# Forget-gate series moved from GpSimd to VectorE, three operand splits moved between GpSimd and VectorE, and queries' parts moved by DMA

## Chip, cores and metric

One core of one Trainium2 chip. The metric is the device time of one execution in microseconds; the median of three runs of the kernel before is 821.5 us (821.19 to 821.72).

## What is computed

One step of a single hybrid encoder layer on 576 tokens: 512 prompt tokens, and 64 sample tokens that also look at a cache of 128. Eight heads use forgetting attention (running sums of log forget gates are added to the scores), eight heads use sparse attention (an indexer chooses the keys). Cut to what matters here:

```python
h = x @ w_in                                  # (576, 1024) @ (1024, 3376)
logf = log_sigmoid(fg + b_f)                  # 8 forget gates per token
cum  = cumsum(logf, axis=1)
# forgetting heads: softmax(q k^T / 8 + cum_q - cum_k, causal) v
# indexer: score = sum_h iw[h] * relu(iq[h] @ ik^T); keep the best topk keys
# sparse heads: softmax(q k^T / 8 over the kept keys) v
x = LN1(ALPHA * x + mix @ w_o)
x = LN2(ALPHA * x + relu(x @ w_up)**2 @ w_down)
y = x + sigmoid(x @ w_g + b_g) * (pe @ w_ple)
# outputs: y, and the new rows k, v, logf, idx_k
```

All matmuls are float32 in precision: each operand is split into a high part and a low part (value less high part), and three products are summed.

## The kernel before

The layer is worked on transposed: model columns lie on the 128 partitions, the 576 tokens along the free axis in two halves of 288. The 16 heads are handled in 8 pairs, p = 0 to 3 of the forgetting kind, p = 4 to 7 of the sparse kind. `proj(p)` projects a pair in the order k, q, v (k of pair 0 is done earlier, with the indexer's projection, in `idx_main`); each of the three is 48 matmuls into one PSUM tile `m`. While pair p+1 is projected, the attention of pair p runs between its matmuls: `drive` steps a main generator (one step is 6 matmuls), and after each step runs due work of `later`, the `fillers`, and a share of a background generator (the `ticks` with the stages `qk`, `addmax`, `exp`, `ptrans`, `pevac`, `pv`, `oevac`).

A weight unit is 128x1024. It is loaded by SP into one of three raw slots (`wraw`, line 163), its high part is made by ScalarE (`whl`, line 182), its low part by VectorE or, where `pool_l` is set, by GpSimd (line 186); a slot is free for the next load when the low parts are done. Each unit has two such pieces of 128x512.

The forget gates: `bg0` is the background of `proj(0)`. It calls `gates` (line 447) and `logf_part` (lines 525 to 547: log sigmoid by an exponential on ScalarE and a polynomial, results in `LF`), waits 8 steps, and calls `cum_part` (line 552: running sums by matmuls on `LF`); 3 steps later `cumT_part` transposes the sums and sends them by `gate_rows` (line 587) into the rows of `KLP` that the scores of `qk` (lines 811 and 813) read.

The indexer runs as a filler from the start of `proj(0)`: `idx_rest` rotates (`idx_rope`, lines 455 to 458), splits keys and queries (`zk_stack`, line 469; `zq_stack`, line 485) and transposes them on TensorE (lines 473, 490; evacuated at 474 and 492). Then `logit_jobs` multiplies head by head (line 601), with ReLU on ScalarE (line 606) and the weighted sum over heads on VectorE (lines 609 and 611). `choice` then selects the keys on VectorE by repeated maximum and replacement of eight (lines 631 and 633).

`proj_evac` evacuates a projection. For a query of p < 4 it makes two operands, QE (partitions 0 to 63 the high part of the even head, 64 to 127 its low part) and QO (the other way round): high parts by ScalarE (lines 680, 681), low parts by VectorE (682, 683), with copies into `Q2` by GpSimd (686, 687). For a key, the high part is moved to the other half by two DMAs (line 714) and the low part goes to `KLP` (lines 717, 718) by GpSimd, for p = 0 by VectorE. `v_out` transposes the values and splits them into `VHL` on GpSimd (lines 752, 753); their output is a DMA on SP (line 747).

Order within an engine: the program is written in the order above and then arranged by the language's scheduler, engine by engine; on the chip each engine, and SP's queue of DMA issues, takes its instructions in that fixed order.

Of the kernel before, what the change touches and what calls it, by code (L numbers as in the profile page):

```python
# [8 lines left out]
F32 = mybir.dt.float32  # L9
# [8 lines left out]
NS = 64  # L18
# [17 lines left out]
def tile_hybrid_step(ctx: ExitStack, tc: tile.TileContext, I, O):  # L36
# [287 lines left out]
    for p in range(8):  # L324
        for x, kind in enumerate("kqv"):
            U[kind, p] = WT.add(qkv[p * 3 + x], pool_l=(x < 2 and p > 1))
# [196 lines left out]
    def logf_part():  # L523
# [5 lines left out]
        w = sb.tile([128, 5, 8], F32, name="lg_w")  # L529
        ACT.activation(e, z, AF.Abs)  # L530
        ACT.activation(e, e, AF.Exp, scale=-1.0)
        DVE.tensor_scalar(w, z, 0.0, None, op0=OP.min)
        DVE.tensor_scalar(t, e, 2.0, None, op0=OP.add)
        DVE.reciprocal(t, t)
        POOL.tensor_tensor(t, t, e, OP.mult)
        POOL.tensor_tensor(t2, t, t, OP.mult)
        POOL.tensor_scalar(t, t, -2.0, None, op0=OP.mult)
        POOL.tensor_scalar(s, t2, 1.0 / 17, None, op0=OP.mult)
        for c in (15, 13, 11, 9, 7, 5, 3):
            POOL.tensor_scalar(s, s, 1.0 / c, None, op0=OP.add)  # L540
            POOL.tensor_tensor(s, s, t2, OP.mult)
        POOL.tensor_scalar(s, s, 1.0, None, op0=OP.add)
        POOL.tensor_tensor(s, s, t, OP.mult)
        POOL.tensor_tensor(LF[:, 0:4], s[:, 0:4], w[:, 0:4], OP.add)
        POOL.tensor_tensor(LF[:NS, 4:5], s[:NS, 4:5], w[:NS, 4:5], OP.add)
# [107 lines left out]
    def proj_evac(p, kind, m):  # L653
# [5 lines left out]
        def q(fn, d=None):  # L659
            if d is not None:  # L660
                dly[0] = d
            later(dly[0], fn)
# [14 lines left out]
        if g == 0:  # L677
            if kind == "q":
                P["q32s"] = sb.tile([128, NS], F32, name="q32s", bufs=2)
                q(lambda: ACT.mul(v2(QE[lo]), v[lo], sc))  # L680
                q(lambda: ACT.mul(v2(QO[hi]), v[hi], sc))
                q(lambda: DVE.scalar_tensor_tensor(v2(QE[hi]), v[lo], sc, f(v2(QE[lo])), op0=OP.mult, op1=OP.subtract))
                q(lambda: DVE.scalar_tensor_tensor(v2(QO[lo]), v[hi], sc, f(v2(QO[hi])), op0=OP.mult, op1=OP.subtract))
                q(lambda: ACT.mul(P["q32s"], m[:, 1, HW - NS:HW], sc))
                P["Q2"] = Q2[p % 2]
                q(lambda: POOL.tensor_copy(P["Q2"][lo, 0], f(QE[lo, :NP])))
                q(lambda: POOL.tensor_copy(P["Q2"][hi, 1], f(QO[hi, :NP])))
# [28 lines left out]
        eng = POOL if p else DVE  # L716
# [25 lines left out]
    def v_out(p):  # L742
# [9 lines left out]
        POOL.tensor_copy(VHL[:, :, :, 0, :], tv)  # L752
        POOL.tensor_tensor(VHL[:, :, :, 1, :], tv, f(VHL[:, :, :, 0, :]), OP.subtract)
# [200 lines left out]
    def bg0():  # L954
# [3 lines left out]
        for _ in range(8):  # L958
            yield 1
# [590 lines left out]
```

## Time and profile before

| | before |
|---|---|
| median of three runs | 821.5 us |
| profiled execution | 821.17 us |
| its span | 819.5 us |
| TensorE matmul busy | 797.4 us, 97% |
| VectorE busy | 569.3 us, 69% |
| ScalarE busy | 453.9 us, 55% |
| GpSimd busy | 131.5 us, 16% |

The span reaches from the first to the last instruction of the profiled execution; 1.7 us of its time lie outside. Engines are called PE (TensorE), DVE (VectorE), ACT (ScalarE), POOL (GpSimd) and SP, whose queue issues the DMAs; PEld is TensorE's loading of weights. L552 is line 552 of the kernel. Matmuls overlap in the pipeline, so a busy TensorE need not be one at its peak; a share of busy time is a mean over stages that have different limits. [...]

### The profile page before, as it was taken

How to read it: one execution, taken by the hardware profiler on the slowest of the kernel's cores; microseconds unless marked ns; L12 is line 12 of the kernel's file. 1: busy time of each engine (PE TensorE's matmuls, PEld its weight loads, DVE VectorE, ACT ScalarE, POOL GpSimd, SP SyncE). 2: the span in 40 equal slices, each digit the busy share in tenths (PEclk: the TensorE clock that was granted, in tenths of full speed). 3: DMA queues.
4: the chain of work that ended last, by engine and by line, in shares of the span. 5: the costliest groups of instructions: out<-in, count | busy, mean ns of one | idle time of the engine just before them, and what ended most of it. 6: DMA issues, size and time to landing. Idle time of an engine off the chain costs nothing.

```text
span 819.5 us, 15103 instructions
## 1 busy us (share of the span) xinstructions
PE 797.4 (97%) x5916; PEld 776.4 (95%) x5916; DVE 569.3 (69%) x1150; ACT 453.9 (55%) x965; POOL 131.5 (16%) x147
## 2 busy tenths in 40 slices
PE   7888999999999999999999999999999999999997
PEld 7877898989999999999999999999999999999997
DVE  6648999996646755889955947658485774737553
ACT  5537766588887954578532625345262543716451
POOL 8414252353350200120000000000000000012200
PEclk9979999999999999999999999999999999999999
DMA  8425122225322322442311414133131422631001
GB/s 290 163 9 137 67 57 87 79 77 195 115 69 73 112 65 78 155 163 83 129 52 54 121 34 142 64 103 100 55 106 52 129 78 83 239 108 48 23 31 64
DMA packets 29255, 79.68 MB, mean 97 GB/s; under 512 B 4864, under 2 KB 8704, under 8 KB 29056
## 3 DMA queue, kind: packets, MB, share of 16 engines
q1 hardware_dynamic: 29184, 78.72, 30.6%
q8 instruction: 46, 0.75, 0.4%
q14 instruction: 25, 0.20, 0.1%
HBM read 66.38 MB, written 9.54 MB: 93 GB/s over the span
## 4 chain that ended last, share of the span: by engine, by line
PE 82%; DVE 13%; ACT 2%; issue 1%; POOL 1%; DMA 1%; DVEq 0%; ACTq 0%
PE g L278 53%; PE m L278 15%; DVE dbias L633 3%; DVE m L631 3%; PE n L278 2%; DVE dbias L611 2%; PE V L897 2%; PE T L64 2%; DVE PT L878 1%; DVE sP L821 1%; PE S L416 1%; PE m L409 1%; PE m L416 1%; DVE whl L186 1%; PE S L813 1%
## 5 line engine op out<-in xcount | busy, mean ns | idle before, releaser
L182 ACT CAST whl<-wraw 128x512 fp32r<-128x512 f32 (+1 forms) x226 | 135.0, 611 | 160.2 <-PE g L278 149.1
L186 DVE TENSOR_TENSOR whl<-wraw,whl 128x512 fp32r<-128x512 f32 (+1 forms) x202 | 137.1, 697 | 68.5 <-ACT whl L182 67.5
L278 PE MATMUL g<-BH,whl 128*128 128x288 f32 (+2 forms) x864 | 181.7, 297 | 0.2 <-DVE Y L1205 0.2
L278 PE MATMUL m<-AH,whl 128*128 128x288 f32 x736 | 181.2, 312 | 0.0
L278 PEld LDWEIGHTS g<-BH,whl 128*128 128x128 f32 x864 | 141.1, 188 | 2.4 <-ACT u L1314 1.1
L278 PEld LDWEIGHTS m<-AH,whl 128*128 128x128 f32 x736 | 128.4, 191 | 1.3
L278 PE MATMUL g<-BL,whl 128*128 128x288 f32 (+2 forms) x432 | 127.2, 295 | 0.0
L278 PE MATMUL m<-AL,whl 128*128 128x288 f32 x368 | 110.4, 300 | 0.0
L278 PE MATMUL g<-hidE,whl 128*128 128x288 f32 (+2 forms) x768 | 103.6, 295 | 0.0
L278 PE MATMUL g<-hidO,whl 128*128 128x288 f32 (+2 forms) x768 | 103.3, 295 | 0.0
L278 PEld LDWEIGHTS g<-hidE,whl 128*128 128x128 f32 x768 | 102.3, 188 | 0.1
L278 PEld LDWEIGHTS g<-hidO,whl 128*128 128x128 f32 x768 | 102.3, 188 | 0.0
L278 PEld LDWEIGHTS g<-BL,whl 128*128 128x128 f32 x432 | 81.3, 188 | 0.1
L278 PEld LDWEIGHTS m<-AL,whl 128*128 128x128 f32 x368 | 70.6, 192 | 0.3
L278 PE MATMUL g<-s,whl 128*128 128x288 f32 x432 | 68.5, 298 | 0.0
L1097 POOL TENSOR_TENSOR ln_s<-Y 128x576 f32<-128x576 f32 (+2 forms) x3 | 4.6, 1546 | 383.7 <-DVE Y L1380 371.3
L278 PEld LDWEIGHTS g<-s,whl 128*128 128x128 f32 x432 | 60.1, 188 | 2.3 <-DVE u L1316 1.2
L829 ACT ACTIVATE sP<-sP,st 128x128 f32<-128x128 f32 (+4 forms) x72 | 39.7, 552 | 37.9 <-DVE st L821 37.7
L1355 DVE SCALAR_TENSOR_TENSOR Y<-Y,g 128x576 f32<-128x576 f32 x48 | 36.0, 751 | 21.6 <-PE g L278 21.1
L278 PE MATMUL m<-BH,whl 128*128 128x288 f32 x192 | 43.7, 304 | 0.0
L878 DVE TENSOR_TENSOR PT<-T,PT 128x128 fp32r<-128x128 f32 (+1 forms) x64 | 31.0, 484 | 16.3 <-ACT PT L877 15.8
L64 PE MATMUL T<-ident,sP 128*128 128x128 f32 (+1 forms) x176 | 31.3, 274 | 5.2 <-DVE PT L878 2.5
(276 smaller groups left out, 1353.5 us busy)
## 6 DMA issues: line engine op xcount, KB each, us to landing
wraw<-in_w_up_dram SPq DMA_DIRECT2D x32, 512.0 KB, 3.5
wraw<-in_w_down_dram SPq DMA_DIRECT2D x32, 512.0 KB, 3.5
wraw<-in_w_qkv_dram SPq DMA_DIRECT2D x23, 512.0 KB, 3.9
wraw<-in_w_gate_dram SPq DMA_DIRECT2D x8, 512.0 KB, 5.1
wraw<-in_w_o_dram SPq DMA_DIRECT2D x8, 384.0 KB, 3.1
out_vT_dram<-v SPq DMA_DIRECT2D x8, 288.0 KB, 2.1
Y<-in_xT_dram SPq DMA_DIRECT2D x8, 288.0 KB, 5.7
PLD<-PL SPq DMA_DIRECT2D x4, 576.0 KB, 2.8
```

The lines of the kernel that those rows point to most:

```text
L64: PE.transpose(out, in_, ident[:n, :n])
L182: ACT.copy(self.hv[h][0], src)
L186: eng.tensor_tensor(lv, src, f(hv), OP.subtract)
L278: PE.matmul(ps, W(w, kw, wc), a[:, ka, cols], start=(first and i == 0), stop=(last and i == n - 1))
L416: PE.matmul(acc[b][:n[b], :304], a[:, k, b * 128:b * 128 + n[b]], ixw(part, k), start=(k == 0 and i == 0), stop=(k == 7 and i == 2))
L611: DVE.scalar_tensor_tensor(dst[:n, :nk], r[:n, :nk], w, dst[:n, :nk], op0=OP.mult, op1=OP.add)
L631: DVE.max(m, s)
L633: DVE.match_replace(out=s, in_to_replace=m, in_values=s, imm_value=GONE)
L829: ACT.activation(j["P"], j["P"], AF.Exp, bias=j["st"][:, 0:1], scale=-1.0, accum_out=s)
L878: DVE.tensor_tensor(t[:, 1, :n, c], v, f(t[:, 0, :n, c]), OP.subtract)
L897: PE.matmul(ps[:, c], w, j["PT"][:, x, kb, c], start=(kb == 0 and x == 0), stop=(kb == i and x == 1))
L1355: later(0, lambda y=y, m=m, s=s: DVE.scalar_tensor_tensor(y, y, s, m[:, :, :HW], op0=OP.mult, op1=OP.add))
```

## The change

- `logf_part`: the absolute value is made on VectorE (a product with -1 and a maximum), not on ScalarE; the polynomial runs on VectorE, with addition and product in one instruction, not on GpSimd; the exponential stays on ScalarE.
- `bg0`: 11 steps instead of 8 before the running sums.
- Low parts of weights: GpSimd makes those of all units from 2q on (q and v of p = 2, all three of p = 3 to 7). Before it was k and q of p = 2 to 7.
- The low parts in `KLP` for p = 1 and the split of the values of p = 0 go from GpSimd to VectorE.
- Queries of p = 1 to 3: one ScalarE operation makes the high parts of both heads on 128 partitions, one VectorE operation the low parts, in the buffers t2 and t1; four DMAs on SP's queue move the quarters to QE and QO. The copies into `Q2` read the new tile.

```diff
@@ -323,7 +323,7 @@
     qkv, wup, wdown = tiles_of("w_qkv", 8), tiles_of("w_up", 8), tiles_of("w_down", 4)
     for p in range(8):
         for x, kind in enumerate("kqv"):
-            U[kind, p] = WT.add(qkv[p * 3 + x], pool_l=(x < 2 and p > 1))
+            U[kind, p] = WT.add(qkv[p * 3 + x], pool_l=(p * 3 + x > 6))
     for j, ap in enumerate(tiles_of("w_o6", 6)):
         U["o", j] = WT.add(ap)
     for k, ap in zip((6, 7), tiles_of("w_o2", 1)):
@@ -526,23 +526,20 @@
         t = sb.tile([128, 5, 8], F32, name="lg_t")
         t2 = sb.tile([128, 5, 8], F32, name="lg_t2")
         s = sb.tile([128, 5, 8], F32, name="lg_s")
-        w = sb.tile([128, 5, 8], F32, name="lg_w")
-        ACT.activation(e, z, AF.Abs)
+        DVE.tensor_scalar(e, z, -1.0, None, op0=OP.mult)
+        DVE.tensor_tensor(e, e, z, OP.max)
         ACT.activation(e, e, AF.Exp, scale=-1.0)
-        DVE.tensor_scalar(w, z, 0.0, None, op0=OP.min)
         DVE.tensor_scalar(t, e, 2.0, None, op0=OP.add)
         DVE.reciprocal(t, t)
-        POOL.tensor_tensor(t, t, e, OP.mult)
-        POOL.tensor_tensor(t2, t, t, OP.mult)
-        POOL.tensor_scalar(t, t, -2.0, None, op0=OP.mult)
-        POOL.tensor_scalar(s, t2, 1.0 / 17, None, op0=OP.mult)
+        DVE.tensor_tensor(t, t, e, OP.mult)
+        DVE.tensor_tensor(t2, t, t, OP.mult)
+        DVE.tensor_scalar(s, t2, 1.0 / 17, None, op0=OP.mult)
         for c in (15, 13, 11, 9, 7, 5, 3):
-            POOL.tensor_scalar(s, s, 1.0 / c, None, op0=OP.add)
-            POOL.tensor_tensor(s, s, t2, OP.mult)
-        POOL.tensor_scalar(s, s, 1.0, None, op0=OP.add)
-        POOL.tensor_tensor(s, s, t, OP.mult)
-        POOL.tensor_tensor(LF[:, 0:4], s[:, 0:4], w[:, 0:4], OP.add)
-        POOL.tensor_tensor(LF[:NS, 4:5], s[:NS, 4:5], w[:NS, 4:5], OP.add)
+            DVE.scalar_tensor_tensor(s, s, 1.0 / c, t2, op0=OP.add, op1=OP.mult)
+        DVE.scalar_tensor_tensor(s, s, 1.0, t, op0=OP.add, op1=OP.mult)
+        DVE.tensor_scalar(e, z, 0.0, None, op0=OP.min)
+        DVE.scalar_tensor_tensor(LF[:, 0:4], s[:, 0:4], -2.0, e[:, 0:4], op0=OP.mult, op1=OP.add)
+        DVE.scalar_tensor_tensor(LF[:NS, 4:5], s[:NS, 4:5], -2.0, e[:NS, 4:5], op0=OP.mult, op1=OP.add)
         with nc.allow_non_contiguous_dma(reason="rows of eight heads"):
             SP.dma_start(O["lf"].rearrange("p (b h) -> p b h", b=5), LF[:, 0:5])
 
@@ -677,14 +674,24 @@
         if g == 0:
             if kind == "q":
                 P["q32s"] = sb.tile([128, NS], F32, name="q32s", bufs=2)
-                q(lambda: ACT.mul(v2(QE[lo]), v[lo], sc))
-                q(lambda: ACT.mul(v2(QO[hi]), v[hi], sc))
-                q(lambda: DVE.scalar_tensor_tensor(v2(QE[hi]), v[lo], sc, f(v2(QE[lo])), op0=OP.mult, op1=OP.subtract))
-                q(lambda: DVE.scalar_tensor_tensor(v2(QO[lo]), v[hi], sc, f(v2(QO[hi])), op0=OP.mult, op1=OP.subtract))
+                P["Q2"] = Q2[p % 2]
+                if p == 0:
+                    q(lambda: ACT.mul(v2(QE[lo]), v[lo], sc))
+                    q(lambda: ACT.mul(v2(QO[hi]), v[hi], sc))
+                    q(lambda: DVE.scalar_tensor_tensor(v2(QE[hi]), v[lo], sc, f(v2(QE[lo])), op0=OP.mult, op1=OP.subtract))
+                    q(lambda: DVE.scalar_tensor_tensor(v2(QO[lo]), v[hi], sc, f(v2(QO[hi])), op0=OP.mult, op1=OP.subtract))
+                    src = (QE, QO)
+                else:
+
+                    qh, ql = [sb.tile([128, NT], F32R, name="qs", tag=t) for t in ("t2", "t1")]
+                    q(lambda: ACT.mul(v2(qh), v, sc))
+                    q(lambda: DVE.scalar_tensor_tensor(v2(ql), v, sc, f(v2(qh)), op0=OP.mult, op1=OP.subtract))
+                    q(lambda: (SP.dma_start(f(QE[lo]), f(qh[lo])), SP.dma_start(f(QO[hi]), f(qh[hi]))))
+                    q(lambda: (SP.dma_start(f(QE[hi]), f(ql[lo])), SP.dma_start(f(QO[lo]), f(ql[hi]))))
+                    src = (qh, qh)
                 q(lambda: ACT.mul(P["q32s"], m[:, 1, HW - NS:HW], sc))
-                P["Q2"] = Q2[p % 2]
-                q(lambda: POOL.tensor_copy(P["Q2"][lo, 0], f(QE[lo, :NP])))
-                q(lambda: POOL.tensor_copy(P["Q2"][hi, 1], f(QO[hi, :NP])))
+                q(lambda: POOL.tensor_copy(P["Q2"][lo, 0], f(src[0][lo, :NP])))
+                q(lambda: POOL.tensor_copy(P["Q2"][hi, 1], f(src[1][hi, :NP])))
                 return
             k32 = sb.tile([128, NT], F32, name="k32", bufs=1)
             q(lambda: ACT.copy(v2(k32), v))
@@ -713,7 +720,7 @@
         q(lambda: ACT.copy(QO[hi], k32[hi]))
         q(lambda: (SP.dma_start(f(QE[hi]), f(QE[lo])), SP.dma_start(f(QO[lo]), f(QO[hi]))))
         q(lambda: SP.dma_start(O["kT"][g, pp], k32))
-        eng = POOL if p else DVE
+        eng = POOL if p > 1 else DVE
         q(lambda: eng.tensor_tensor(KL[lo, 0], k32[lo, :NP], f(QE[lo, :NP]), OP.subtract))
         q(lambda: eng.tensor_tensor(KL[hi, 1], k32[hi, :NP], f(QO[hi, :NP]), OP.subtract))
         q(lambda: ACT.copy(P["k32s"], k32[:, NP:]))
@@ -749,8 +756,9 @@
         P["VHL"] = VHL
         ACT.copy(vt[:, 0:4], m.rearrange("p (b c) -> p b c", c=128))
         tv = vt[:, 0:4].rearrange("p b (h d) -> p b h d", h=2)
-        POOL.tensor_copy(VHL[:, :, :, 0, :], tv)
-        POOL.tensor_tensor(VHL[:, :, :, 1, :], tv, f(VHL[:, :, :, 0, :]), OP.subtract)
+        eng = POOL if p else DVE
+        eng.tensor_copy(VHL[:, :, :, 0, :], tv)
+        eng.tensor_tensor(VHL[:, :, :, 1, :], tv, f(VHL[:, :, :, 0, :]), OP.subtract)
         yield 1
         yield 1
         yield 1
@@ -955,7 +963,7 @@
 
         gates()
         logf_part()
-        for _ in range(8):
+        for _ in range(11):
             yield 1
         cum_part()
         for _ in range(3):
```

## Rows read from the trace of the kernel before

**Rows 1.** page part 1: engine, busy us, share of the span, instructions

```profile
PE 797.4 (97%) x5916; PEld 776.4 (95%) x5916; DVE 569.3 (69%) x1150; ACT 453.9 (55%) x965; POOL 131.5 (16%) x147
```

**Rows 2.** waits of PE, 28 to 185 us: total us, times, longest

```profile
PE T L552 <- POOL LF L545: 4.4, 1, 4.4
...
PE T L64 <- DVE st L821: 1.9, 2, 1.4
```

**Rows 3.** windows: stretch, length, PE, PEld, DVE, ACT, POOL busy, clock, DMA

```profile
64.00:85.00 21.00, 18.17 (x125) 16.57 (x123) 19.54 (x47) 16.22 (x40) 11.01 (x10) 1.00 0.47 127
85.00:113.90 28.90, 26.96 (x198) 24.29 (x198) 28.27 (x88) 20.69 (x57) 9.42 (x8) 1.00 0.28 86
113.90:145.60 31.70, 30.16 (x234) 28.83 (x233) 30.96 (x88) 20.51 (x54) 12.83 (x13) 1.00 0.23 76
145.60:177.50 31.90, 30.69 (x238) 29.36 (x237) 31.17 (x79) 21.44 (x54) 10.96 (x12) 1.00 0.20 64
...
209.30:239.10 29.80, 29.80 (x233) 28.78 (x232) 17.77 (x43) 24.60 (x60) 11.10 (x10) 1.00 0.26 79
```

**Rows 4.** timeline of POOL, first and last of the 22: start, length, instruction

```profile
34.19 0.27 POOL L535 TENSOR_TENSOR lg_t<-lg_t,lg_e 128x40 f32<-128x40 f32 x1 [10.63 <-ACT kstack L468]
...
43.30 0.20 POOL L545 TENSOR_TENSOR LF<-lg_s,lg_w 64x8 f32<-64x8 f32 x1
```

**Rows 5.** windows around the stall, columns as in group 3

```profile
34.00:38.90 4.90, 4.58 (x37) 4.27 (x35) 4.87 (x13) 2.86 (x10) 3.98 (x10) 1.00 0.02 7
38.90:43.50 4.60, 0.26 (x3) 0.12 (x1) 1.70 (x5) 0.97 (x3) 3.67 (x14) 0.93 0.02 5
43.50:49.70 6.20, 6.14 (x28) 6.13 (x29) 1.81 (x4) 1.92 (x5) 1.18 (x3) 0.50 0.02 3
```

**Rows 6.** timeline of DVE and PE, 32 to 62 us

```profile
32.86 0.18 DVE L533 TENSOR_SCALAR lg_t<-lg_e 128x40 f32<-128x40 f32 x1
32.95 0.75 DVE L458 TENSOR_TENSOR idxs<-idxs,work 128x576 f32<-128x576 f32 x1
...
34.24 0.43 DVE L469 TENSOR_TENSOR kstack<-idxs,kstack 128x64 fp32r<-128x64 f32 x2
...
34.59 0.42 PE L473 MATMUL T<-identr,kstack 128*128 128x128 f32 x2 [0.32 <-DVE kstack L469]
...
47.80 0.69 DVE L492 CAST Z<-S 128x512 fp32r<-128x512 f32 x1 [7.16 <-PE S L490]
...
61.72 0.31 PE L811 MATMUL S<-kE,qE 128*128 128x128 f32 x1
```

**Rows 7.** DVE groups, L611, 70 to 78, 78 to 85 us; POOL timeline

```profile
L611 DVE SCALAR_TENSOR_TENSOR dbias<-work,iw,dbias 128x384 f32<-128x384 f32 x5 | 6.5, 1308 | 0.0
...
L611 DVE SCALAR_TENSOR_TENSOR dbias<-work,iw,dbias 128x384 f32<-128x384 f32 x2 | 1.2, 605 | 0.0
...
70.83 3.14 POOL L186 TENSOR_TENSOR whl<-wraw,whl 128x512 fp32r<-128x512 f32 x2
...
81.69 1.29 POOL L186 TENSOR_TENSOR whl<-wraw,whl 128x512 fp32r<-128x512 f32 x1 [4.49 <-ACT whl L182]
```

**Rows 8.** groups of DVE, 85 to 105 us: count, busy us, mean ns, idle

```profile
L186 DVE TENSOR_TENSOR whl<-wraw,whl 128x512 fp32r<-128x512 f32 x2 | 1.3, 670 | 0.0
...
L682 DVE SCALAR_TENSOR_TENSOR qE<-m,qE 64x576 fp32r<-64x576 f32 x1 | 0.8, 751 | 0.0
```

**Rows 9.** timelines of SP and PE, DMA issues (KB, us to landing)

```profile
110.07 0.50 SPq L714 DMA_DIRECT2D kE<-kE  x1
...
122.04 0.33 SPq L163 DMA_DIRECT2D wraw<-in_w_qkv_dram  x1
...
128.89 0.35 SPq L747 DMA_DIRECT2D out_vT_dram<-v  x1
...
130.36 0.22 PE L811 MATMUL S<-kE,qE 128*128 128x128 f32 x1
...
kO<-kO SPq DMA_DIRECT2D x8, 144.0 KB, 2.7
```

## The prediction

> **What bounds the kernel now.** I read the busy shares first: TensorE is busy 97% of the span [rows 1], so a change can only win where TensorE waits or runs slowly. The waits of TensorE between 28 and 185 us come next [rows 2]: one wait of 4.4 us for line 545 stands above all others, which are small and name VectorE. Then the table by stage [rows 3]: from 177 us on a head pair takes 29.8 us with TensorE never idle, whereas the pairs before take 31.7 and 31.9 us with VectorE busy about 98%. So there are two places with something to win. Place one is the stall at 39 us. Place two is 64 to 177 us, where TensorE is idle 2.8 + 1.9 + 1.5 + 1.2 = 7.4 us (stretch less busy time, four rows of [rows 3]). Behind 177 us TensorE is the bound and nothing in the change takes work from it, so what is won before 177 us stays won to the end, and nothing is added there.
>
> The stall explains itself in the GpSimd's timeline [rows 4]: the 22 small operations of the forget gate run from 34.19 to 43.50 us, 0.42 us each, and the running sums at line 552, next in TensorE's order, need their last result. TensorE arrives 4.4 us earlier [rows 2], at 39.1 us. [...]
>
> **Part one, the forget gate's series.** It goes from GpSimd to VectorE. The fused form needs 18 VectorE instructions where 3 stood; 15 are new, 22 on GpSimd and one on ScalarE go. The price of one on a 128x40 tile: the add at line 533 lasts 0.18 us, and the next instruction starts 0.09 us after it [rows 6]. That start-to-start distance is the lower bound (15 x 0.09 = 1.4 us); the upper bound is GpSimd's pace (15 x 0.42 = 6.3 us). I take 0.22, the 0.18 with a little for each result being waited for, since it is the same engine and tile: 15 x 0.22 = 3.3 us.
>
> [...]
>
> When is the result there? VectorE begins at about 33 us and ends near 37, or at 39.3 at the upper price. TensorE now comes three steps later: 18 matmuls at 0.128 us (29.8 us over 233, [rows 3]) is 2.3 us, so about 41.4 us. At either price the wait for line 545 is gone, 4.4 us, and with it the half clock, 3.1 us: together 7.5 us. The sums are needed again by the first scores, at 61.72 us before [rows 6], some 57 us without the stall. From 41.4 us that leaves over 10 us for two small transposes three steps on, their evacuation and a DMA like line 714's (0.5 us to issue, 2.7 to land, [rows 9]), so I cost the three steps at nothing; each us beyond that cover would cost one.
>
> What is late next is VectorE's own work. Up to 40.6 us it has no gap, and TensorE already waits for it once: the transpose at line 473 stood 0.32 us until line 469 was done [rows 6]. The 3.3 us of the series stand ahead of the indexer's operations (the rotations, lines 469 and 485), on which TensorE's transposes wait in order. The 7.16 us of idle VectorE before 47.80 [rows 6] are no cover: they exist because TensorE stood still. So I charge the whole 3.3 us. Bounds: 0, if matmuls of the projection are put ahead of the transposes, and 6.3. **Sum of part one: 7.5 - 3.3 = 4.2 us.**
>
> **Part two, GpSimd free during the head sums** (64 to 85 us). VectorE's accumulations at line 611 on 128x384 take 1.31 us from 70 to 78 us, five of them, and 0.605 us after 78 us [rows 7]. In just that stretch GpSimd runs subtractions such as the two at line 186, 1.57 us each where others take 1.29 [rows 7]. So both are slowed: 5 x 0.70 = 3.5 us of VectorE. The change takes these subtractions away and gives them to VectorE: two low parts of weight 2k, two of KL for p=1, and copy and difference of VHL for p=0. That is 6 operations at 0.67 us (line 186, [rows 8]) = 4.0 us (the copy may be half that). VectorE gains 3.5 and pays 4.0, so I set this part at 0. Bounds: TensorE's idle 2.8 us won, or, if GpSimd's next weight subtractions (81.69 us before) come to lie on the 128x512 accumulations, some 2 us lost.
>
> [...] If the slowing had another cause, the 3.5 us would not come back and the time would be about 3.5 us higher.
>
> **Part three, queries and values.** For p = 1 to 3 two ScalarE and two VectorE operations on 64 partitions become one each on 128; VectorE saves one of 0.75 us (line 682, [rows 8]) per pair. The low parts of weights v, p = 2 to 7, go to GpSimd: 2 x 0.67 = 1.3 us less on VectorE per pair. GpSimd has room: 11 to 13 us of work in 32 [rows 3]. So VectorE is relieved of 2.1 us in each of three stages (85 to 113.9, 113.9 to 145.6, 145.6 to 177.5 us), which exceed what TensorE's own work needs by idle time 1.9 and, from 29.8, by 1.9 and 2.1 us. With 2.1 less, VectorE would still have about 28.9 of 29.8 us to do, and waits on single results remain; I take 1.0 + 1.2 + 1.2 = **3.4 us**. Bounds 0 and 5.9.
>
> Against it stand four DMAs per pair on SP's queue. For p=2, SP waits for a raw slot until 122.04 us [rows 9]; behind that load, four issues at 0.5 us (the like one of line 714 takes 0.50, [rows 9]) end at 124.4, landing takes 2.7 us: 127.1. The first scores of that pair start at 130.36 us [rows 9]. The cover is 3.3 us, so I cost it at nothing. If it were gone, each us late would stall TensorE by one us in three stages. The value pieces on GpSimd release the raw slot 0.6 us later each (1.29 against 0.67), which that cover holds. The buffers t1 and t2, which the parts now use, are wanted again by the next value projection a projection of 48 matmuls (6.1 us and more) on.
>
> **Sum.** 4.2 + 0 + 3.4 = 7.6 us off the profiled execution's 821.17 us: **813.5 us**. That execution lies 0.3 us below the median of 821.5, which is nothing beside the bounds.
>
> **Rivals.**
> 1. *The matmuls hide the series.* If TensorE's order is filled with projection matmuls while VectorE computes, the 3.3 us cost nothing, and half of the 64 to 85 us idle may go as well: 821.2 - 7.5 - 1.4 - 3.4 = 808.9 us. For: TensorE's order interleaves transposes with matmuls. Against: VectorE has no gap before 40.6 us, and from 34 to 38.9 us, when nothing stalls, it is busy 4.87 of 4.90 us while TensorE is busy 4.58 [rows 5].
> 2. *The wait changes its name.* The series makes a stall of 3.3 us at the transposes, and half clock follows as at 43.5 us: part one brings 1.1, total 4.5: 816.7 us. The same comes if part one is right but VectorE's relief after 85 us doesn't reach TensorE: 821.2 - 4.2 = 817.0. Both: 820.1, no change. For: line 473's wait. Against: a wait of 1.4 us for line 821 [rows 2], at 72 us, left the clock at 1.0 [rows 3].
> 3. *Slower: the queries' DMAs are queued behind a later SP wait.* If they stand behind the value output at 128.89 us [rows 9] instead of the load at 122.04, issue ends at 131.2 and they land at 133.9, 3.6 us after the first scores want them; in three stages that is 10.7 us, and the clock may halve on top. 821.2 - 7.6 + 10.7 = 824.3 us. It decides from 3.3 us of lateness. Against: the program has them a whole projection ahead of that output.
>
> **How the numbers follow.** A measurement here can tell about 0.2%, 1.6 us. Forecast, 811 to 816 us: 0.40. Rival 1, 806 to 811: 0.18. Rival 2, one of its forms, 816 to 819.9: 0.20; both forms or gains and losses that cancel, 819.9 to 823.1: 0.10. Rival 3, or disorder of its kind: 0.12. So faster 0.78, same 0.10, slower 0.12. The range 807 to 820.5 leaves out a little of rival 1 and all of rival 3.
>
> **What would show it.** Step one: no TensorE wait for LF, clock 1.0 between 40 and 50 us, and instead up to some 3 us of waits for kstack or the indexer's query parts (lines 469, 485). Step two: line 611 on 128x384 at 0.6 us throughout. Step three: pairs 1 and 2 near 30.5 us between their BL operations, and no wait of lines 811 and 813 for a DMA. The prediction is wrong if clock 0.5 shows up in a new place, if TensorE waits for the queries' DMAs, or if the time from 64 to 85 us grows.

## The result, and the profile after

The median went from 821.35 us (821.18 to 821.72, four executions) to **811.37 us** (811.03 to 811.54, four executions). The ratio is 0.9877, with a 95% interval of 0.9860 to 0.9895: 10.0 us less, where 7.6 us were forecast. The profiled execution took 811.2 us, its span is 809.5 us.

The page of the kernel after: the busy times that stood in [rows 1] (engine, busy us, share, instructions), and TensorE's granted clock in 40 slices, in tenths of full speed (9 is 90% or more).

```profile
PE 791.1 (98%) x5916; PEld 770.7 (95%) x5916; DVE 562.3 (69%) x1156; ACT 450.4 (56%) x961; POOL 131.1 (16%) x131
PEclk9999999999999999999999999999999999999999
```

TensorE does the same 5916 matmuls in 6.3 us less busy time: most of the difference is work that before went at a low clock or haltingly, not work that is gone. The waits of TensorE from 28 to 185 us in the kernel after (total us, times, longest), to be read against [rows 2]:

```profile
PE T L64 <- DVE PT L886: 2.7, 3, 1.5
PE V L896 <- DVE mix L923: 2.6, 3, 1.0
PE T L473 <- DVE kstack L469: 0.6, 2, 0.3
```

The wait of 4.4 us for the forget gates (`LF`) is gone and no wait of its size has come; the small ones for `mix` grew from 1.2 to 2.6 us in all. The table by stage of the kernel after has the columns of [rows 3] (stretch, length, busy time and count of PE, PEld, DVE, ACT, POOL, then clock, DMA share and GB/s). The first two rows lie where the last two of [rows 5] lay, the third holds the indexer's short transposes, the rest are the stages up to the end of pair 2.

```profile
38.90:43.50 4.60, 4.28 (x33) 3.69 (x32) 4.54 (x16) 4.53 (x12) 1.35 (x2) 1.00 0.00 2
43.50:49.70 6.20, 6.20 (x51) 6.20 (x52) 5.30 (x12) 2.28 (x7) 0.00 (x0) 1.00 0.29 88
50.20:53.20 3.00, 2.97 (x24) 2.36 (x24) 2.37 (x5) 1.88 (x7) 0.00 (x0) 1.00 0.45 126
54.00:75.00 21.00, 20.19 (x139) 18.47 (x139) 19.86 (x46) 18.34 (x48) 4.86 (x6) 1.00 0.63 101
75.00:103.60 28.60, 25.38 (x189) 22.99 (x189) 27.86 (x93) 18.79 (x53) 10.24 (x10) 1.00 0.37 107
103.60:135.20 31.60, 29.88 (x232) 28.55 (x231) 30.82 (x90) 19.87 (x53) 15.40 (x15) 1.00 0.33 97
135.20:167.50 32.30, 31.29 (x243) 29.95 (x242) 31.27 (x87) 20.93 (x53) 13.46 (x13) 1.00 0.25 79
```

From 38.9 to 43.5 us TensorE is now busy 4.28 us, where it was busy 0.26; from 43.5 to 49.7 us the clock is 1.00, full speed, where it was 0.50, and 51 matmuls start there instead of 28. The two head pairs in the last rows last 31.6 and 32.3 us, as long as before (31.7 and 31.9, [rows 3]). The end of a pair is marked by GpSimd's operation for `BL`; its start in the two kernels:

| end of pair | 0 | 1 | 2 | 3 |
|---|---|---|---|---|
| before, us | 113.92 | 145.57 | 177.45 | 206.33 |
| after, us | 103.58 | 135.18 | 167.50 | 196.28 |
| earlier by, us | 10.34 | 10.39 | 9.95 | 10.05 |

So the whole gain is there by the end of pair 0, and nothing is won or lost behind it. The last matmul of the index projection starts at 29.62 us before and at 30.54 us after; from there to the end of pair 0 it is 84.30 us before and 73.04 us after, **11.3 us less, of which the later start takes back 0.9**. That start lies between 29.62 and 31.17 us in the fourteen profiled executions of this document, the kernel before being the earliest, and kernels whose edits to the kernel after concern later work only lie there at either side of it (e6 29.80, e11 31.17, after 30.54); so the 0.9 us look like scatter between executions and not like an effect of the change, but no kernel's profile was repeated to show it.

The part of the gain that the prediction had no term for stands in two rows of the kernel before that it didn't look at. Its table by stage, between the half clock and the first scores:

```profile
54.60:59.50 4.90, 4.90 (x22) 3.30 (x22) 2.09 (x5) 2.03 (x6) 0.00 (x0) 1.00 0.54 23
59.50:63.40 3.90, 3.90 (x20) 3.90 (x20) 1.50 (x6) 1.78 (x6) 0.00 (x0) 0.56 0.71 47
```

TensorE's timeline before, ahead of them and in the first of them (start, length, operation, tile, rows times columns):

```profile
52.37 0.22 PE L490 MATMUL S<-identr,fox 128*128 128x128 f32 x1
...
52.62 0.22 PE L490 MATMUL S<-identr,fox 128*128 128x128 f32 x1
...
55.41 0.25 PE L490 MATMUL S<-identr,fox 64*128 64x64 f32 x1
55.59 0.40 PE L278 MATMUL m<-AL,whl 128*128 128x288 f32 x1
55.92 0.25 PE L490 MATMUL S<-identr,fox 64*128 64x64 f32 x1
```

TensorE's timeline after, from the arrival of `LF` to the first scores:

```profile
43.41 0.28 PE L473 MATMUL T<-identr,kstack 128*128 128x128 f32 x1 [0.27 <-DVE kstack L469]
...
43.86 0.31 PE L549 MATMUL T<-LF,tri 128*128 128x48 f32 x2
...
51.11 0.48 PE L490 MATMUL S<-identr,fox 64*128 64x64 f32 x4
51.52 0.40 PE L278 MATMUL m<-AH,whl 128*128 128x288 f32 x1
...
52.50 0.49 PE L490 MATMUL X<-identr,fox 64*128 64x64 f32 x4
...
54.18 0.33 PE L819 MATMUL S<-kE,qE 128*128 128x128 f32 x1
```

Before, the eight transposes on 64 partitions (line 490) alternate one by one with matmuls on 128, one such pair per 0.51 us (55.41, 55.92). A matmul alone takes some 0.13 us of that (29.8 us over 233, [rows 3]). Alternating by itself costs less: the transposes on 128 partitions just ahead of them alternate with such matmuls too, at 0.25 us a pair (52.37, 52.62). After, the eight stand in two groups of four, each group done 0.41 or 0.43 us after its first start (51.11 to 51.52, 52.50 to 52.93). That stretch lasts 3.0 us instead of 4.9, with 24 matmuls in it instead of 22. Behind it, before, comes a stretch at a mean clock of 0.56 (0.50 from 59.95 to 63.30 us), although TensorE is recorded as busy all the time ahead of it and in it; after, the clock is 1.00. The first scores start at 54.18 us instead of 61.72 [rows 6].

The ledger of the two profiled executions from the end of the index projection to the end of pair 0:

| what | us |
|---|---|
| wait for `LF`, 4.4, less the new wait of 0.27 at line 473 | 4.1 |
| half clock, 43.5 to 49.7 us: half of 6.2 | 3.1 |
| alternating transposes: 4.9 less 3.0 | 1.9 |
| clock 0.56, 59.5 to 63.4 us: 0.44 of 3.9 | 1.7 |
| together | 10.8 of 11.3 |

The rest is about what TensorE's idle time became less: 4.0 us from 54.0 to 103.6 us after (0.81 + 3.22), 4.8 us in the two stages from 64.0 to 113.9 us before [rows 3].

The last row of the ledger is what one trace shows, not a price that every execution is shown to pay. Eight executions of the kernel before had a mean granted clock of 0.993 over their span, as the profiled one, and twelve had 0.996. That is 0.003 of 820 us, some 2.5 us of clock, yet both groups took 821.1 us on the mean.

### The profile page after: what moved, and what is told of

The parts are those of the page before. It is cut to its first block, busy times and chain, and to the rows that moved or that the text cites. A ratio compares the mean times of both kernels' runs of the same rounds, so it can differ in the third digit from the quotient of the medians.

```text
span 809.5 us, 15121 instructions
## 1 busy us (share of the span) xinstructions
PE 791.1 (98%) x5916; PEld 770.7 (95%) x5916; DVE 562.3 (69%) x1156; ACT 450.4 (56%) x961; POOL 131.1 (16%) x131
## 4 chain that ended last, share of the span: by engine, by line
PE 79%; DVE 10%; issue 5%; ACT 3%; DMA 1%; POOL 1%; SPq 0%; DVEq 0%; ACTq 0%; POOLq 0%
PE g L278 54%; PE m L278 13%; PE n L278 2%; DVE dbias L630 2%; PE V L905 2%; PE T L64 2%; DVE m L628 2%; DVE dbias L608 1%; DVE PT L886 1%; DMA iraw<-in_w_idx_dram 1%; PE S L819 1%; ACT whl L182 1%; PE S L821 1%; ACT xr L703 1%; DMA wraw<-in_w_up_dram 1%
## 5 line engine op out<-in xcount | busy, mean ns | idle before, releaser
L278 PE MATMUL m<-AH,whl 128*128 128x288 f32 x736 | 177.8, 308 | 0.0
L186 DVE TENSOR_TENSOR whl<-wraw,whl 128x512 fp32r<-128x512 f32 (+1 forms) x192 | 130.7, 701 | 65.1 <-ACT whl L182 63.9
L278 PEld LDWEIGHTS m<-AH,whl 128*128 128x128 f32 x736 | 126.5, 188 | 1.1
L186 POOL TENSOR_TENSOR whl<-wraw,whl 128x512 fp32r<-128x512 f32 x34 | 44.2, 1300 | 61.5 <-ACT whl L182 52.2
```

Of the source, the lines that this page charges most:

```text
L186: eng.tensor_tensor(lv, src, f(hv), OP.subtract)
L278: PE.matmul(ps, W(w, kw, wc), a[:, ka, cols], start=(first and i == 0), stop=(last and i == n - 1))
```

## The experiments

Theory A was: the gain is the stall with what hangs on it, the series costs VectorE next to nothing, and VectorE's relief in the pairs is used up by something else. Theory B was the prediction's: the series costs TensorE some 3.3 us, and the relief in the pairs pays that back. All times are medians; a ratio is to the kernel before on the same chip.

**The series alone, and all but the series.** e1_series_only is the kernel before with the new `logf_part` and 11 steps; e2_no_series is the kernel after with the old `logf_part` and 8 steps. The edit of e2:

```diff
-        DVE.tensor_tensor(t, t, e, OP.mult)
+        POOL.tensor_tensor(t, t, e, OP.mult)
...
-            DVE.scalar_tensor_tensor(s, s, 1.0 / c, t2, op0=OP.add, op1=OP.mult)
+            POOL.tensor_scalar(s, s, 1.0 / c, None, op0=OP.add)
+            POOL.tensor_tensor(s, s, t2, OP.mult)
...
-        for _ in range(11):
+        for _ in range(8):
```

> Part one alone: the forget gate's series on VectorE and the running sums three steps later; GpSimd's and the queries' work as before. Theory A (the series fits between VectorE's other instructions and costs it next to nothing, so part one brings the stall, the half clock and the calmer stretch behind it, and nearly all of the gain): 811 to 813.5 us. Theory B (the prediction's sum: the series costs its 3.3 us, parts two and three bring the rest): 817.2 us. The trace under A: no TensorE wait for LF, clock 1.0 from 40 to 64 us.

> Parts two and three alone: the series on GpSimd again and the running sums at their old place. Theory A: the 4.4 us wait and the clock of 0.50 are back, 819.5 to 821.5 us. Theory B: 821.4 - 3.4 = 818.0 us.

e1 took 812.16 us (ratio 0.9893, 0.9878 to 0.9907), 8.95 us less than before. e2 took 819.46 us (0.9980, 0.9971 to 0.9989), 1.65 us less. So part one alone brings nearly everything, and parts two and three alone bring little. The waits of TensorE in e2 still begin with the old one:

```profile
PE T L552 <- POOL LF L545: 4.4, 1, 4.4
```

In e1 the table by stage has clock 1.00 from 28 to 66 us, over the place of the stall and the one of the short transposes, which are grouped here too. Further on, behind two waits of 1.35 and 0.65 us (at 80.43 and 81.39 us), it has a low clock that the kernel after doesn't have (third row):

```profile
28.00:40.00 12.00, 11.71 (x89) 11.38 (x88) 9.97 (x30) 7.71 (x23) 0.12 (x1) 1.00 0.39 124
40.00:66.00 26.00, 24.98 (x178) 22.09 (x177) 22.23 (x58) 18.28 (x50) 4.47 (x5) 1.00 0.41 52
...
82.00:86.00 4.00, 4.00 (x20) 3.75 (x20) 3.74 (x16) 1.74 (x6) 0.00 (x0) 0.59 0.08 29
```

That is 0.41 of 4.0 = 1.6 us in the profiled execution. Two executions of e1 at a mean clock of 0.997 took 812.57 and 813.19 us, the two at 0.999 took 811.27 and 811.75, which is the time of the kernel after. Theory A holds: 8.95 us is over twice the 4.2 us that the prediction gave to part one.

**The three steps.** e3_early_sums is the kernel after, e4_steps_only the kernel before, each with this line changed (e3 to 8, e4 to 11):

```diff
-        for _ in range(11):
+        for _ in range(8):
```

> The changed kernel with 8 steps instead of 11 before the running sums. If the three steps are needed: in the changed kernel LF is ready at 43.5 us and TensorE comes to it at 43.8, so three steps (2.3 us) earlier it waits some 2 us, 813.5 us, and up to 816.5 if the clock halves again. If the scheduler sets the place of the sums by when it expects LF, whatever the steps: 811 to 812 us, the same as the changed kernel.

> The kernel before with 11 steps instead of 8 before the running sums; the series stays on GpSimd. Theory A: LF at 43.5 us as before, TensorE comes some 3 us later than it did, so 1 to 2 us of wait stay and the clock may stay at 1.0: 814 to 818 us. Theory B (what counts is that the wait goes): 821.4 - 2.3 = 819.1 us, or 816 if the half clock goes too. If the steps alone do as much as the whole change, 811 to 812, moving the series was not needed.

e3 took 811.39 us (0.9883, 0.9868 to 0.9897), the same as after: with the series on VectorE the arranged order of TensorE is nearly the same at 8 and at 11 steps. The sums start at 43.34 us in e3, behind a wait of 0.5 us, and at 43.86 us in the kernel after, without one. e4 took 816.39 us (0.9945, 0.9929 to 0.9962), 4.7 us less than before. In its waits a shorter stall is left:

```profile
PE T L552 <- POOL LF L545: 1.1, 1, 1.1
```

And in its table by stage the low clock behind it is milder and shorter:

```profile
46.00:50.00 4.00, 4.00 (x22) 3.87 (x21) 1.84 (x5) 1.54 (x4) 0.05 (x1) 0.58 0.56 152
```

The stall is 3.3 us shorter, and the low clock costs 0.42 of 4.0 = 1.7 us instead of 3.1: together 4.7 us, the difference of the medians. That it comes out so exactly is in part chance. The second low clock of the kernel before, 1.7 us, is missing in e4 as well (the clock is 1.00 from 54 to 70 us, although the short transposes alternate), and with it the sum is 6.4. In the two profiled executions the stretch from the end of the index projection to the end of pair 0 is indeed 6.1 us shorter (78.18 against 84.30), with a start 0.6 us later. So the steps alone are worth about half of the gain when the series stays on GpSimd, and nothing when it has moved.

**The price of the stall, and what lies beyond it.** e10_short_on_gpsimd leaves out 14 of the GpSimd's operations in the kernel before, so that `LF` comes early without VectorE doing any of it. e12_short_gpsimd_late does the same with 11 steps.

```diff
-        for c in (15, 13, 11, 9, 7, 5, 3):
+        for c in ():
             POOL.tensor_scalar(s, s, 1.0 / c, None, op0=OP.add)
...
-        for _ in range(8):
+        for _ in range(11):      # e12 only
```

> The kernel before with the seven polynomial steps (14 GpSimd operations) left out, so that the gates are less exact; nothing else is changed, the sums keep their place, VectorE gets nothing. LF is ready about 5.7 us sooner, near 37.8 us, and TensorE doesn't wait at 39.1. It prices the stall with all its consequences. Prediction's price (4.4 of wait and 3.1 of half clock): 821.4 - 7.5 = 813.9 us. If the slow stretch from 54 to 64 us (clock 0.59 from 60 to 64) is one more consequence: 811 to 812.5 us.

> The kernel before with the seven polynomial steps left out on GpSimd (the gates are less exact) and the running sums three steps later; VectorE gets nothing. In its program the eight 64-partition transposes of the last block still alternate one by one with matmuls, as in the kernel before; where the series is on VectorE they stand in two groups of four. If the alternation and the low clock behind it are the rest of part one's gain: no better than the short series at the old place, 813.5 to 815 us. If the three steps bring the rest: 811.5 to 812.5 us.

e10 took 814.55 us (0.9916, 0.9897 to 0.9935), 6.9 us less than before: the price that the prediction set on stall and half clock was 7.5. What is still missing against after shows in its table by stage:

```profile
48.30:53.20 4.90, 4.90 (x23) 3.35 (x23) 2.15 (x5) 2.35 (x6) 0.00 (x0) 0.99 0.53 23
53.20:58.20 5.00, 5.00 (x30) 5.00 (x30) 1.45 (x6) 2.17 (x7) 0.00 (x0) 0.66 0.73 44
```

The short transposes alternate as before and take 4.90 us, and a low clock follows, 0.34 of 5.0 = 1.7 us. Three executions of e10 with a mean granted clock of 0.995 to 0.997 took 814.4 to 815.4 us, the one at 1.000 took 813.48. That one stands 2.1 us above after, close to the 1.9 us of the alternating transposes; it is a single execution.

e12 took 812.88 us (0.9896, 0.9877 to 0.9915). Four of its five executions, at clock 0.999 to 1.000, took 812.64 to 813.02; the profiled one was slowed to 0.52 from 53 to 59 us, with no wait of TensorE from 40 to 60 us, and took 817.59. Its transposes alternate, too. Neither expectation was met: at full clock the three steps bring about 0.6 us (813.48 to 812.88), and about 1.5 us are left to after. That this rest is the order of the transposes is argued from the 1.9 us of the windows; an order of transposes changed by itself was not tried.

**The price of the series.** e7_short_series leaves out six of the polynomial's instructions on VectorE in the kernel after.

```diff
-        for c in (15, 13, 11, 9, 7, 5, 3):
+        for c in (3,):
             DVE.scalar_tensor_tensor(s, s, 1.0 / c, t2, op0=OP.add, op1=OP.mult)
```

> The changed kernel with six of the seven steps of the polynomial left out, so that the log forget gates are less exact; six VectorE instructions fewer. Theory A (they cost VectorE little and TensorE nothing): 811.0 to 811.7 us. Theory B (each costs 0.22 us on TensorE's path): 811.4 - 1.3 = 810.1 us.

e7 took 810.97 us (0.9874, 0.9859 to 0.9890), 0.4 us less than after, with intervals that nearly coincide. The prediction's 0.22 us each would have made it 1.3, which the spread of its executions (810.29 to 812.92) doesn't exclude by itself. The two traces speak against it: from the end of the index projection to the end of pair 0 e7 takes 73.22 us and the kernel after 73.04, so nothing is won there. The reason is in VectorE's timeline of the kernel after:

```profile
37.75 0.19 DVE L538 SCALAR_TENSOR_TENSOR lg_s<-lg_s,lg_t 128x40 f32<-128x40 f32 x1
37.86 0.75 DVE L457 TENSOR_TENSOR idxs<-idxs,rope 128x576 f32<-128x576 f32 x1
38.52 0.20 DVE L538 SCALAR_TENSOR_TENSOR lg_s<-lg_s,lg_t 128x40 f32<-128x40 f32 x1
...
40.03 0.62 DVE L538 SCALAR_TENSOR_TENSOR lg_s<-lg_s,lg_t 128x40 f32<-128x40 f32 x1
...
41.60 0.61 DVE L538 SCALAR_TENSOR_TENSOR lg_s<-lg_s,lg_t 128x40 f32<-128x40 f32 x1
...
43.37 0.15 DVE L542 SCALAR_TENSOR_TENSOR LF<-lg_s,lg_e 64x8 f32<-64x8 f32 x1
```

The series is interleaved one by one with other work, so no link of the chain stands directly behind the one whose result it needs, and from its start to the next start it is 0.11 us (37.75 to 37.86). Two of the chain, at 40.03 and 41.60 us, take 0.54 and 0.63 us to the next start. Added up in this way the 15 new instructions take 2.7 us of VectorE. The result comes late, at 43.5 us, and TensorE comes for it at 43.86 us. In between TensorE is given projection matmuls.

Another reason would be that VectorE's other work runs faster once GpSimd no longer computes beside it. The rotations don't show it: lines 457 and 458 take 0.76 and 0.77 us in the kernel before while the series runs on GpSimd (at 35.88 and 37.24 us), and 0.75 and 0.76 us in the kernel after.

**GpSimd free in the head sums.** e6_no_part2 gives GpSimd back what part two took from it, in the kernel after:

```diff
-            U[kind, p] = WT.add(qkv[p * 3 + x], pool_l=(p * 3 + x > 6))
+            U[kind, p] = WT.add(qkv[p * 3 + x], pool_l=(p * 3 + x > 5))
...
-        eng = POOL if p > 1 else DVE
+        eng = POOL if p else DVE
...
-        eng = POOL if p else DVE
+        eng = POOL
```

> The changed kernel with the low part of weight 2k, KL of p = 1 and VHL of p = 0 on GpSimd again. Theory A (the head sums are slowed again while GpSimd runs subtractions, and VectorE is rid of 4.0 us: nothing in all): 810.9 to 812.4 us. Theory B (the slowed sums delay the scores, on which TensorE waits): 813 to 814.5 us. In the trace line 608 on 128x384 should be near 1.3 us where GpSimd runs, 0.61 elsewhere.

e6 took 811.42 us (0.9876, 0.9861 to 0.9891): part two is worth nothing in the whole time. VectorE's groups of head sums, first in the kernel after (tile, count, busy us, mean ns, idle before):

```profile
L608 DVE SCALAR_TENSOR_TENSOR dbias<-work,iw,dbias 128x512 f32<-128x512 f32 x7 | 6.3, 896 | 0.0
L608 DVE SCALAR_TENSOR_TENSOR dbias<-work,iw,dbias 128x384 f32<-128x384 f32 x7 | 4.3, 613 | 0.0
```

And in e6:

```profile
L608 DVE SCALAR_TENSOR_TENSOR dbias<-work,iw,dbias 128x512 f32<-128x512 f32 x7 | 7.4, 1062 | 0.0
L608 DVE SCALAR_TENSOR_TENSOR dbias<-work,iw,dbias 128x256 f32<-128x256 f32 x7 | 4.4, 635 | 0.8 <-ACT work L603 0.3
```

My expectation of 1.3 us on 128x384 in e6 missed, they take 0.61 there too: since the head sums come earlier now, GpSimd's work meets other forms of them, 128x512 and 128x256. The four forms together take 19.4 us in e6 as they did before, and 17.6 us in after.

By stage the nothing is a loss and a gain. From the end of the index projection to the end of pair 0 e6 takes 75.11 us, 2.1 more than after, and VectorE spends 19.8 us there on the key selection, 16.4 in after. In return the selection ends earlier in e6, at 161.9 us, 5 us before the end of pair 2, and that pair takes 30.55 us instead of 32.3:

```profile
104.90:136.40 31.50, 30.24 (x236) 28.91 (x234) 30.71 (x87) 20.00 (x53) 15.41 (x14) 1.00 0.34 97
136.40:166.95 30.55, 29.97 (x234) 28.71 (x233) 28.56 (x85) 21.46 (x55) 13.51 (x13) 1.00 0.26 77
```

So the work that part two gives to VectorE displaces selection to later stages, and TensorE waits there instead. This rests on one profiled execution of each kernel, both at clock 1.00 in these stages.

**The queries' parts and the values' low parts.** In the kernel after, e11_no_dmas takes back the queries' block and with it the DMAs; e5_no_part3 takes back this and the values' low parts.

```diff
-            U[kind, p] = WT.add(qkv[p * 3 + x], pool_l=(p * 3 + x > 6))
+            U[kind, p] = WT.add(qkv[p * 3 + x], pool_l=(x < 2 and p * 3 + x > 6))   # e5 only
...
-                    q(lambda: ACT.mul(v2(qh), v, sc))
-                    q(lambda: DVE.scalar_tensor_tensor(v2(ql), v, sc, f(v2(qh)), op0=OP.mult, op1=OP.subtract))
...
+                q(lambda: DVE.scalar_tensor_tensor(v2(QE[hi]), v[lo], sc, f(v2(QE[lo])), op0=OP.mult, op1=OP.subtract))
+                q(lambda: DVE.scalar_tensor_tensor(v2(QO[lo]), v[hi], sc, f(v2(QO[hi])), op0=OP.mult, op1=OP.subtract))
```

> The changed kernel with the queries' parts made and placed as before (no DMAs) and the values' low parts of the weights on VectorE again; parts one and two stay. Theory A (VectorE's freed 2.1 us per pair are filled with steps of the key selection, and TensorE waits as long as ever): 811 to 812 us, no change from 811.4. Theory B (the prediction: part three brings 3.4 us): 814.8 us.

> The changed kernel with the queries' parts made in place as before, without the twelve DMAs; the values' low parts of the weights stay on GpSimd. If the DMAs cost what the saved VectorE operation brings: 811 to 811.8 us. If they delay scores: 810 us or less. If the one operation is worth its 0.75 us per pair: 813.5 us.

e5 took 811.01 us (0.9868, 0.9852 to 0.9885), e11 812.03 us (0.9882, 0.9861 to 0.9903; 810.13 us for its execution at clock 0.999, 811.9 to 812.7 for those at 0.997 and 0.998). Neither can be told from after. The two pairs of e5 in its table by stage:

```profile
102.10:134.20 32.10, 30.07 (x234) 28.75 (x233) 31.33 (x92) 21.18 (x55) 12.71 (x12) 1.00 0.26 80
134.20:166.30 32.10, 30.87 (x240) 29.59 (x240) 31.44 (x78) 20.56 (x52) 10.95 (x12) 1.00 0.20 62
```

They last what they last in after, 64.2 against 63.9 us, and VectorE is as full. The relief of 2.1 us a pair is real, but it is filled at once: in those two pairs the key selection (its two lines, 628 and 630) holds VectorE for 43.2 us in after, for 38.5 us before and for 39.4 us in e5, and its last step comes at 168.66, 182.65 and 184.45 us. Its total is the same in all three, 61.3 to 61.5 us. The two lines in the two pairs, first in after, then before:

```profile
sum 63.90, DVE 20.41; mean DVE 10.20
...
sum 63.90, DVE 22.77; mean DVE 11.38
...
sum 63.60, DVE 18.18; mean DVE 9.09
...
sum 63.60, DVE 20.34; mean DVE 10.17
```

**What VectorE's fill costs.** e9_half_selection leaves out half of the selection's rounds in the kernel after; e8_slow_choice lowers the rate at which the program feeds selection steps.

```diff
-            for r in range(16 if i < 4 else 6):
+            for r in range(8 if i < 4 else 3):       # e9
...
-    state = {"choice": None, "chosen": 0, "k": 0.0, "rate": 0.65, "logits": False}
+    state = {"choice": None, "chosen": 0, "k": 0.0, "rate": 0.58, "logits": False}   # e8
```

> The changed kernel with half of the selection's rounds left out (8 for 16, 3 for 6 in the sample's block), so that fewer keys are marked; VectorE is rid of some 25 us of work. Theory A (TensorE's waits in pairs 0 to 2 stand where VectorE's order has selection steps between, and any VectorE time set free is filled with them): with too few steps to fill, pairs 1 and 2 fall from 31.6 and 32.3 towards 29.8 to 30.5 us and the time to 806 to 809 us. Theory B (the waits come from the chain score, exponential, transpose itself): 811 to 811.7 us.

> The changed kernel with the indexer's steps handed out at a rate of 0.58 a step instead of 0.65, so that fewer selection steps stand among the work of each head pair. Theory A (the selection fills VectorE, and TensorE's waits on VectorE in pairs 1 and 2 come from it): the pairs shorten from 31.6 and 32.3 towards 30.5 us and the time goes to 809 to 810.5 us, unless the head sums or the selection end too late, then 813 or more. If the filling doesn't matter: 811.4.

e9 took 807.29 us (0.9829, 0.9809 to 0.9849), 4.1 us less than after. The same two pairs in its table by stage:

```profile
103.40:133.40 30.00, 30.00 (x234) 28.89 (x234) 22.76 (x68) 21.15 (x56) 15.45 (x15) 1.00 0.34 97
133.40:162.70 29.30, 29.30 (x230) 28.28 (x229) 12.23 (x35) 19.97 (x51) 13.44 (x13) 1.00 0.28 79
```

TensorE is never idle in them, and they fall to the 29 to 30 us of its own work. So the pairs are held up by what stands ahead in VectorE's order, and the selection is the part of it that can be elsewhere; nothing else about the pairs needed to change. Pair 2 of e6, without selection in its last 5 us, is a weaker sign of the same with the whole work done.

e8 missed: I had expected a gain, and it took 813.94 us (0.9904, 0.9889 to 0.9919), 2.6 us more than after. The selection still ended early, at 172.85 us, so the rate hardly thins it. Another arrangement brought low clocks instead, in its table by stage:

```profile
50.00:60.00 10.00, 10.00 (x58) 8.86 (x58) 4.37 (x13) 4.33 (x14) 0.00 (x0) 0.83 0.62 33
...
75.00:106.00 31.00, 28.12 (x189) 25.29 (x188) 29.57 (x91) 19.76 (x55) 9.77 (x9) 0.89 0.27 82
```

The first lies where the short transposes of e8 come, in groups of two and singly. The clock is 0.17 of 10.0 us and 0.11 of 31.0 us, 1.7 and up to 3.4 us, more than the 2.6 us lost. So e8 doesn't say what a slower feed is worth at full clock.

Of all these, no kernel with the whole work is measurably better than the one after; e5 (811.01 us) does the same with no DMAs for the queries.

## Why the prediction was right, and where not

The time came 2.1 us under the forecast of 813.5, inside its range and inside the forecast's own stretch of 811 to 816. Some terms were right, others missed in both directions.

- **Stall and half clock, 7.5 us: right.** The table by stage has 4.1 and 3.1 us, and e10, which shortens the series and gives VectorE nothing to do, gains 6.9. The 3.1 us of the sum are half of the 6.20 us at clock 0.50 in [rows 5], which come behind 4.60 us with TensorE busy for 0.26. What showed it was named beforehand: no wait for `LF`, clock 1.00 from 40 to 50 us, and a small wait for kstack (line 473) in its place, 0.3 us instead of up to 3.
- **The series, charged 3.3 us: mis-sized, it is next to nothing for TensorE.** Six of its instructions gone win 0.4 us by the medians and nothing by the traces (e7), and TensorE is busy 4.28 of 4.60 us while most of the series runs. The step that failed is "I charge the whole 3.3 us": VectorE's time doesn't reach TensorE, because projection matmuls stand in its order in the meantime, the mechanism of rival 1. I had given the zero as a bound and argued it away with VectorE's being full; that VectorE is full doesn't say that TensorE waits. The price on VectorE itself was nearly met, 2.7 us, but for another reason than mine. The 0.22 us was a whole duration plus waiting, whereas an undisturbed instruction of the chain takes 0.11 us, near the lower bound of 0.09. The little that I had added for each result being waited for had no case here, since other work stands between; what two links directly behind each other would cost no run shows. Most of the rest of the 2.7 us are the two instructions that lasted until GpSimd's copies were done (0.54 and 0.63 us, last section).
- **When the result is there: wrong, and harmless.** I had said 37 to 39.3 us; it is 43.5, as late as on GpSimd [rows 4]. TensorE comes 0.4 us later. So the cover was not the more than two microseconds that I had worked out, but next to nothing; the arrangement put the sums just where the result is. And the three steps, costed at nothing as moved work, turned out to bring nothing (e3).
- **A term that I didn't have: 3.6 us.** I took the low clock to end with the stretch of [rows 5] and read no row between 49.7 and 64 us. The alternating transposes (1.9) and the low clock behind them (1.7 in the profiled execution) were there to be seen. The order, grouped or alternating, follows the place of the series: grouped where VectorE has it (after and seven of its kin), alternating where GpSimd has it (before, e2, e4, e10, e12); e8, with the series on VectorE, has both. Why the arrangement comes out so is not shown.
- **Part two, 0 us: right in size** (e6), for smaller sums than mine. The head sums became 1.8 us cheaper (19.4 to 17.6), not 3.5: on 128x384 they are 0.61 us throughout, as I had said, but GpSimd's next subtractions now lie on the 128x512 ones (0.74 us each before, 0.90 after). That was the mishap given as the loss bound. Nor was it only a sum on VectorE that came out even: part two wins about 2 us up to the end of pair 0 and loses about as much in pairs 1 and 2 (e6), which the prediction had not seen. The right size is luck.
- **Part three, 3.4 us: wrong, it is 0** (e5, e11). The pairs were to fall near 30.5 us and stayed at 31.6 and 32.3. I had treated relief of a full engine as a gap that stays open. The arrangement fills it with the next ready work, 4.7 us more of selection in the two pairs, and TensorE waits as long as before; only e9, where that work doesn't exist, gets both pairs to 29 to 30 us.
- **Rivals.** Rival 1 (808.9) named the right reason for the series but had part three's 3.4 us in it. Without them and with the term of 3.6 it would be 821.2 - 7.5 - 1.4 - 3.6 = 808.7, and the later start of 0.9 us brings that to 809.6. Rival 2 failed in its first form; its second, "VectorE's relief doesn't reach TensorE", is what happened in the pairs. Rival 3 did not come. In SP's timeline of the kernel after the four issues lie ahead of the load, not behind the values' output at 118.34 us:

```profile
108.82 0.50 SPq L689 DMA_DIRECT2D qE<-qs  x1
...
111.43 0.59 SPq L690 DMA_DIRECT2D qO<-qs  x1
112.11 0.54 SPq L163 DMA_DIRECT2D wraw<-in_w_qkv_dram  x1
```

Issued by 112.0 and landed 2.9 us later (the median of the queries' DMAs), they are there 5 us before the first scores of that pair, at 120.06 us.

So 10.0 was met with 7.6 because errors partly cancel: 3.3 us charged for the series and 3.6 not seen, 6.9 too low; 3.4 us for part three and 0.9 for the later start, 4.3 too high. That leaves 2.6, against the 2.4 measured. The mechanism of part one's gain was right; that the time came so near to the forecast is luck. (The last step of its sum is rounded down: 821.17 less 7.6 is 813.6.)

What stays open: parts two and three alone bring 1.65 us while the stall is there (e2), whereas each taken back from after costs nothing that can be measured. They don't add up, and no run takes both back other than e1, whose 812.16 us cannot be told from after. In its profiled execution e2 lacks the second low clock of the kernel before (1.00 from 54 to 75 us), and 1.7 us is the size of its gain; but since the kernel before took the same time at a mean clock of 0.993 and 0.996, that is not shown to be the reason.

## What to carry to other kernels

Price a stall with everything behind it up to the first row at full clock and full pace, and read each row on the way, also those in which the engine is "busy": here 3.6 us stood in two such rows. A small operation that landed among others on the full VectorE cost its distance of starts here (0.11 us), not its duration (0.19), but 0.54 and 0.63 us beside a copy on GpSimd; TensorE, with projection matmuls in its order meanwhile, was busy 4.28 of 4.60 us. The relief of VectorE by 2.1 us a pair was worth nothing here (the two pairs take 63.9 us with it and 64.2 without, e5), because other ready work was arranged into the place: first see what would move in.

## What the runs showed of the hardware

- **The clock fell without idle time.** In the kernel before, 0.56 from 59.5 to 63.4 us came behind 4.9 us in which TensorE was recorded busy throughout, with short transposes and matmuls alternating and 22 matmuls instead of the 40 of the 4.9 us before; in e10, 0.66 likewise. In the eight profiled executions with grouped transposes the clock is 1.00 from 28 to 75 us. Alternation alone doesn't decide it: in e2 and e4 the clock behind it is 1.00. Nor do waits: in e4 one of 1.1 us was followed by 0.58, in e1 two of 1.35 and 0.65 us by 0.59, whereas single waits of up to 1.5 us in the kernel after, whose stages up to 167 us all show 1.00, left no trace in it. And the same program doesn't always get it: e12 took 812.6 to 813.0 us in four executions at 0.999 to 1.000 and 817.6 in one at 0.996. What makes the clock fall these runs don't settle.
- **Short transposes alternating with matmuls took longer than in a row.** A transpose on 64 partitions and a matmul on 128 take 0.51 us as an alternating pair in the kernel before (55.41 to 55.92 us), a transpose on 128 partitions and such a matmul 0.25 us (52.37 to 52.62); four of the short transposes in a row take 0.41 us in the kernel after (51.11 to 51.52). Where in the alternation the time goes no run here shows.
- **A tiny VectorE operation took three times its length beside a copy on GpSimd.** Two of the series' instructions on 128x40 took 0.62 and 0.61 us instead of 0.19, at 40.03 and 41.60 us. Those are the moments of two copies, in GpSimd's timeline of the kernel after:

```profile
39.99 0.61 POOL L693 CAST fox<-qE 64x512 fp32r<-64x512 f32 x1 [15.24 <-ACT qE L679]
41.41 0.74 POOL L694 CAST fox<-qO 64x512 fp32r<-64x512 f32 x1 [0.81 <-ACT qO L680]
```

Each of the two ends shortly after the copy, at 40.65 and 42.21 us against 40.60 and 42.15. They are the only operations of GpSimd between 39 and 43 us, and the other instructions of the polynomial's chain (line 538) took 0.19 or 0.20 us. That the short operation waited for the long one is read from these two endings; no run moves the copies alone.
